# Masked attention: another key block for GpSimd, its product later, and five places instead of four

## The chip, the cores and the metric

The kernel runs on one core of a Trainium2 chip. The metric is the device time of one execution in microseconds (us). Of the kernel before there are three timed runs, with a median of 1539.09 us (1537.86 to 1539.81), and one more execution that was profiled.

The engines by the names of the profile: PE is the matrix engine (PEld its weight loads), DVE the vector engine, ACT the scalar engine, POOL the GpSimd engine, SP the engine that issues most transfers. Each works through its instructions in the order in which they were written out for it.

## The reference

One layer of a diffusion transformer over 1024 latent tokens of width 1024, with 256 context tokens beside them. Two attention branches run on the same tokens: A is windowed (each query sees keys at most 128 tokens away) and B is global; both see all context keys, both have 8 query heads in 2 groups of 4 that share a key head. The change is in A:

```
scores = where(mask, q @ k.T / 8, -inf)      # a block of 128 queries, 3 x 128 keys around it, 256 context keys
m = max(max(scores), sink)
e = exp(scores - m);  p = e / (sum(e) + exp(sink - m))
out = p @ v
```

After the branches come a gated merge, an output projection, a layer norm, a convolutional SwiGLU feed-forward part and a second layer norm. Everything is computed to single precision.

## The kernel before

**Numbers in two parts.** A matrix product takes its operands in a rounded 32-bit form. To keep single precision, a number x is split into a high part (x rounded) and a low part (x minus the high part), and products are summed over the parts.

**Units.** The attention is cut into 32 units: branch (0 is A, 1 is B), block i of 128 queries, key head g. A unit of A in the middle of the sequence has five key blocks of 128: three of the window, and two of the context (numbers 0 to 4); the units of the first and last query block have four. In names, `0_3_1` is branch 0, query block 3, key head 1; `ptl0_3_1_2` is the low part of its block 2.

**A unit's stages.** First scores (`lat`, L507): for each of four heads PE writes scores and mask to PSUM (tile `s`, two places), DVE negates them, bounds them by the sink and finds the maximum (L545), and ACT takes the exponential (L547). One unit later come the values (`value_steps`, L595): one step for each key block. A step (`tr_step`) transposes the block of probabilities for four heads on PE (L604, tile `ptr`, one of three PSUM places of kind `pt` that it shares with two other transposes) and splits it into a high part `pth` and a low part `ptl`. Three steps later (`LAG`), PE multiplies the values with the high part (L627) and with the low part (L628, `av_step`); all blocks of a unit add up in one PSUM place `av`. When the last is in, `out_step` follows: ACT copies `av` out (L639), POOL moves one half (L640), DVE adds the halves (L643), POOL scales the sum (L646) and splits it into the output's two parts (`O`, L84 and L87).

**Who splits a block.** Normally ACT writes the high part from PSUM (L615) and DVE the low part (L616). For the blocks named in `POOL_LO`, ACT copies the block from PSUM to one of two side buffers (L612) and POOL does both parts from there (L84, L87 by way of `split`). In A this holds for one block of each of the eleven units 1_0 to 6_0, block 3 before. Such a block's product is due `PLAG` steps later than the usual three. POOL also splits the queries of a coming unit (`qs`, L84 and L87; it waits there for PE's transpose of an earlier `qs`, L486) and writes a small column (L542).

**What sets the order.** The program lists steps by a table; a scheduler in the language's layer then sets each engine's order from it, and gives tiles their places. `pth` and `ptl` have four places each; a fifth block can only be written when the product of the one that held the place is done. `av_issue` puts the products that are due behind each step.

Of the kernel before, what the change touches and what calls it, by code (L numbers as in the profile page):

```python
# [8 lines left out]
R32 = mybir.dt.float32r  # L9
# [4 lines left out]
P = 128  # L14
# [12 lines left out]
ALPHA = 2.0 ** 0.25  # L27
HALF = 512
FBIG = 3.0e38
POOL_LO = (3,), (2, 6)  # L30
PLAG = 1, 2
VL = 1
NXT = 17
LAG = 3, 3
# [35 lines left out]
def layer_kernel(  # L70
# [9 lines left out]
    def split(src, hi, lo, hi_eng, lo_eng):  # L80
        if hi_eng is nc.scalar:
            nc.scalar.copy(hi, src)  # L82
        elif hi_eng is nc.gpsimd:
            nc.gpsimd.tensor_scalar(out=hi, in0=src, scalar1=1.0, scalar2=0.0, op0=ALU.mult, op1=ALU.add)  # L84
        else:
            hi_eng.tensor_copy(hi, src)
        lo_eng.tensor_tensor(out=lo, in0=src, in1=hi.bitcast(F32), op=ALU.subtract)  # L87
# [378 lines left out]
    class Unit:  # L466
# [128 lines left out]
        def value_steps(self):  # L595
            nm, kt = self.id, self.kt
            vh = self.br * 2 + self.g
            last = self.id == f"1_{NT - 1}_1"
            parts = {}

            def tr_step(n):
                tr = pt_tile(f"ptr{nm}_{n}", R32)
                for h in range(4):
                    i = nc.tensor.transpose(tr[:, h * P:(h + 1) * P], self.bits[:, h, n * P:(n + 1) * P], identr)  # L604
                    tc.add_manual_dep(i.ins, self.owner, data, reason="the row's words are read under another type")
                tr = tr.bitcast(F32)
                hi = att.tile([P, 512], R32, tag="pth", name=f"pth{nm}_{n}", bufs=4)
                lo = att.tile([P, 512], R32, tag="ptl", name=f"ptl{nm}_{n}", bufs=4)
                pooled = n in POOL_LO[self.br] and not last and (self.br or 2 <= 2 * self.i + self.g < 2 * NT - 3)
                if pooled:  # L610
                    rw = side_tile()
                    nc.scalar.copy(rw, tr)  # L612
                    split(rw, hi, lo, nc.gpsimd, nc.gpsimd)
                else:
                    nc.scalar.copy(hi, tr)  # L615
                    nc.vector.tensor_tensor(out=lo, in0=tr, in1=hi.bitcast(F32), op=ALU.subtract)  # L616
                parts[n] = hi, lo
                return pooled

            def av_step(n):  # L620
                first = self.left == len(kt)
                self.left -= 1
                if first:
                    self.av = ps2.tile([P, 512], F32, tag="av", name=f"av{nm}")
                hi, lo = parts.pop(n)
                v = VT[kt[n] // 2][:, kt[n] % 2, vh]
                nc.tensor.matmul(self.av, v, hi, start=first, stop=False)  # L627
                nc.tensor.matmul(self.av, v, lo, start=False, stop=self.left == 0)  # L628

            def out_step():  # L630
                av = self.av
                up = att.tile([HD, 512], F32, tag="up", name=f"up{nm}", bufs=1)
                ot = att.tile([P, 2, P], F32, tag="ot", name=f"ot{nm}", bufs=1)
                if last:
                    low = av
                    nc.scalar.copy(up, av[HD:P])
                else:
                    low = side_tile()
                    nc.scalar.copy(low, av)  # L639
                    nc.gpsimd.tensor_scalar(out=up, in0=low[HD:P], scalar1=1.0, scalar2=0.0, op0=ALU.mult, op1=ALU.add)  # L640
                oe = nc.gpsimd if (self.br or self.i >= NT - 2) and not last else nc.vector
                for h in range(2):
                    oe.tensor_tensor(out=ot[h * HD:(h + 1) * HD],  # L643
                                     in0=low[0:HD].rearrange("p (a b q) -> p a b q", b=2, q=P)[:, :, h],
                                     in1=up.rearrange("p (a b q) -> p a b q", b=2, q=P)[:, :, h], op=ALU.add)
                (nc.vector if last else nc.gpsimd).tensor_tensor(out=ot, in0=ot, in1=self.rb, op=ALU.mult)  # L646
                hf = self.i // 4
                qs = slice((self.i % 4) * P, (self.i % 4 + 1) * P)
                split(ot, otile(self.br, hf, 0, self.g)[:, :, qs], otile(self.br, hf, 1, self.g)[:, :, qs],
                      *((nc.scalar, nc.vector) if last else (nc.gpsimd, nc.gpsimd)))  # L650

            def step(ns):
                pooled = [tr_step(n) for n in ns]
                for n, pl in zip(ns, pooled):
                    clk[0] += 1
                    avq.append((self, n, clk[0] + LAG[self.br] + (PLAG[self.br] if pl else 0)))
                    av_issue()

            self.left = len(kt)
            self.av_step, self.out_step = av_step, out_step  # L660
            g = 1 + self.br
            steps = [lambda n=n: step(range(n, n + g)) for n in range(0, len(kt), g)]
            steps.insert(3 if self.br else 2 if self.i else len(steps), self.rows)
            return steps
# [155 lines left out]
    for n, (gi, k) in enumerate(order):  # L820
# [19 lines left out]
        nm, src, tiles = groups[gi]  # L840
# [40 lines left out]
    def otile(br, hf, hl, g):  # L881
        key = br, hf, hl, g
        if key not in O:
            O[key] = opool.tile([P, 2, HALF], R32, tag="O", name="O%d%d%d%d" % key, bufs=12)
        return O[key]

    att = tc.alloc_tile_pool(name="att", bufs=1, side="right", reuse_waits="tile")
    ps2 = tc.alloc_tile_pool(name="ps2", bufs=1, space=PSUM, reuse_waits="tile")

    def pt_tile(name, dt=F32):  # L890
        return ps2.tile([P, 512], dt, tag="pt", name=name, bufs=3)
# [13 lines left out]
    def side_tile():  # L905
        turn[0] ^= 1
        return side[:, turn[0]]
# [8 lines left out]
    def av_issue(flush=False):  # L916
        while avq:
            u = avq[0][0]
            c = [e for e in avq if e[0] is u and (flush or e[2] <= clk[0])]
            if not c:  # L920
                return
            e = min(c, key=lambda e: e[2])
            avq.remove(e)
            u.av_step(e[1])
            if u.left == 0:
                u.out_step()
# [170 lines left out]
    for f in range(2, KT):  # L1097
# [4 lines left out]
        for hs in halves:  # L1102
            n = HALF * len(hs)
# [246 lines left out]
    for f in (4, 6):  # L1350
        for si in (1, 2):
# [3 lines left out]
            elif f == 6:  # L1355
                (_, st), (_, dg), (_, ca), *ap = ln1(si)
                n = len(pend) - 4
# [587 lines left out]
```

## Time and profile before

| what | us |
|---|---|
| timed runs, median (lowest to highest) | 1539.09 (1537.86 to 1539.81) |
| the profiled execution, its own time | 1537.76 |
| its span, from the first to the last instruction | 1536.0 |
| PE busy in the span | 1507.2 |
| DVE, ACT, POOL busy | 1176.7, 788.3, 749.5 |
| PE idle from 362 to 451 us, where the units with a POOL block are | 9.69 |

The span is 1.76 us shorter than the execution's own time. Branch A's units run from about 333 to 466 us, branch B's to about 733 us; before are projections and gates, after are merge, projection and feed-forward. The matrix clock is granted fully throughout (0.998 in the mean).

A row of the profile's timeline has start, duration, engine, line, operation, out and in, shape, count, and in brackets the idle time ahead of it with what ended that. A row of a group has `| busy, mean ns | idle ahead <- what ended it`. A row of waits has `engine line waited for: us in total, times, longest`. In a row of windows, each engine's busy time stands in the order PE, PEld, DVE, ACT, POOL, then the clock, the transfers' share and GB/s.

### The profile page before, as it was taken

What the parts mean: (1) busy time and instruction counts of PE and PEld (TensorE: products, weight loads), DVE (VectorE), ACT (ScalarE), POOL (GpSimd) and SP (SyncE); (2) the same over time, 40 slices, a digit from 0 to 9 for tenths busy, and PEclk for the clock granted to TensorE, in tenths of its full rate; (3) what the DMA queues carried; (4) which work ended last, traced back from release to release, by engine and by line L of the source; (5) the groups of instructions that cost most, each with busy time, mean ns of one, the idle gap of its engine ahead of it and who ended that gap; (6) DMA issues with size and microseconds to landing.
All of it is one profiled execution on the core that took longest, in us unless ns stands there. A gap on an engine that the chain in (4) does not pass through costs nothing.

```text
span 1536.0 us, 22204 instructions
## 1 busy us (share of the span) xinstructions
PE 1507.2 (98%) x7804; PEld 1263.5 (82%) x7804; DVE 1176.7 (77%) x1761; ACT 788.3 (51%) x1303; POOL 749.5 (49%) x727
## 2 busy tenths in 40 slices
PE   9999999999899999999999999999999999999997
PEld 7888888887777888887888998888888888888887
DVE  6677986638788778878765888888888888657884
ACT  5322222448888777777333554444444444435552
POOL 0356522415667677766123436666667774121121
PEclk9999999999999999999999999999999999999999
DMA  9777672312223677663550322333344447996731
GB/s 371 267 242 247 205 254 87 119 61 70 63 81 82 159 166 154 153 145 87 209 165 24 111 87 96 111 110 110 110 110 110 111 110 229 339 273 210 249 105 55
DMA packets 114399, 232.09 MB, mean 151 GB/s; under 512 B 13200, under 2 KB 28048, under 8 KB 114192
## 3 DMA queue, kind: packets, MB, share of 16 engines
q1 hardware_dynamic: 99056, 201.82, 39.5%
q0 software_dynamic: 10400, 20.19, 8.7%
q10 hardware_dynamic: 4832, 8.68, 1.5%
q8 instruction: 61, 1.00, 0.3%
q14 instruction: 50, 0.41, 0.1%
HBM read 179.45 MB, written 65.86 MB: 160 GB/s over the span
## 4 chain that ended last, share of the span: by engine, by line
PE 88%; POOL 5%; DVE 2%; issue 2%; ACT 2%; DMA 0%; SPq 0%; DVEq 0%; POOLq 0%; ACTq 0%
PE p L90 4%; PE p L91 4%; PE p L92 4%; PE g L90 4%; PE g L91 4%; PE g L92 4%; PE ptr L604 4%; PE av L628 3%; PE av L627 3%; PE b L90 3%; PE b L92 3%; PE b L91 3%; PE c L90 2%; PE c L92 2%; PE d L92 2%; PE c L91 2%
## 5 line engine op out<-in xcount | busy, mean ns | idle before, releaser
L616 DVE TENSOR_TENSOR ptl<-ptr,pth 128x512 fp32r<-128x512 f32 x195 | 128.5, 684 | 28.3 <-ACT pth L615 26.9
L547 ACT ACTIVATE p<-p,nm 128x1280 f32<-128x1280 f32 (+2 forms) x128 | 139.5, 1091 | 12.9 <-DVE p L545 11.9
L615 ACT CAST pth<-ptr 128x512 fp32r<-128x512 f32 x195 | 110.9, 589 | 46.6 <-PE ptr L604 40.3
L87 DVE TENSOR_TENSOR ld<-rd,hd 128x1024 fp32r<-128x1024 f32 x77 | 94.9, 1249 | 51.7 <-ACT hd L82 49.5
L82 ACT CAST hd<-rd 128x1024 fp32r<-128x1024 f32 x77 | 79.4, 1050 | 83.0 <-PE p L92 57.7
L604 PEld LDWEIGHTS ptr<-identr,pb 128*128 128x128 f32 x944 | 97.3, 141 | 21.2 <-ACT pb L550 3.1
L628 PE MATMUL av<-ptl,VT 128*128 128x512 f32 x236 | 98.5, 417 | 10.6 <-POOL ptl L87 10.4
L87 POOL TENSOR_TENSOR wlg<-wg,whg 128x512 fp32r<-128x512 f32 x32 | 48.0, 1510 | 122.2 <-ACT whg L82 83.0
L604 PE MATMUL ptr<-identr,pb 128*128 128x128 f32 x944 | 105.2, 243 | 1.8 <-ACT pb L550 1.2
L90 PE MATMUL p<-hd 128*128 128x512 f32 x264 | 103.5, 392 | 0.0
L627 PE MATMUL av<-pth,VT 128*128 128x512 f32 x236 | 102.2, 433 | 1.2 <-ACT side L639 0.8
L91 PE MATMUL p<-ld,hd 128*128 128x512 f32 x264 | 102.9, 390 | 0.0
L92 PE MATMUL p<-hd,ld 128*128 128x512 f32 x264 | 102.8, 389 | 0.0
L90 PE MATMUL g<-hh,whg 128*128 128x512 f32 x256 | 99.9, 390 | 0.0
L92 PE MATMUL g<-hh,wlg 128*128 128x512 f32 x256 | 99.7, 389 | 0.0
L91 PE MATMUL g<-hl,whg 128*128 128x512 f32 x256 | 99.7, 389 | 0.0
L545 DVE TENSOR_SCALAR_CACHE_REDUCE p<-s,cvt,nmc 128x1024 f32<-128x1024 f32 x64 | 84.0, 1315 | 8.1 <-PE s L497 8.1
L496 PE MATMUL s<-KL,q 128*128 128x512 f32 (+2 forms) x192 | 74.7, 389 | 1.2 <-DVE p L545 1.2
L497 PE MATMUL s<-KL,q 128*128 128x512 f32 (+2 forms) x192 | 72.0, 375 | 0.0
L783 ACT ACTIVATE sg<-g,bgc 128x512 f32<-128x512 f32 x32 | 22.0, 686 | 96.2 <-PE g L92 96.2
L82 ACT CAST wS<-s 128x512 fp32r<-128x512 f32 x76 | 45.3, 620 | 47.5 <-POOL s L1244 46.7
L82 ACT CAST wA<-ru 128x512 fp32r<-128x512 f32 x57 | 35.5, 623 | 63.8 <-PE d L92 34.9
(438 smaller groups left out, 4877.8 us busy)
## 6 DMA issues: line engine op xcount, KB each, us to landing
wml<-in_wmodT_dram SPq DMA_DIRECT2D x48, 512.0 KB
ru<-in_w_up_dram SPq DMA_DIRECT2D x38, 512.0 KB
rd<-td SPq DMA_DIRECT2D x55, 256.0 KB
rd<-sd SPq DMA_DIRECT2D x44, 256.0 KB
rd<-in_w_dn_dram SPq DMA_DIRECT2D x33, 256.0 KB
wm<-in_wmodT_dram SPq DMA_DIRECT2D x16, 512.0 KB
wg<-in_w_g_dram SPq DMA_DIRECT2D x32, 256.0 KB
sgd<-sg ACTq DMA_DIRECT2D x32, 256.0 KB
```

The source lines that it names most:

```text
L82: nc.scalar.copy(hi, src)
L87: lo_eng.tensor_tensor(out=lo, in0=src, in1=hi.bitcast(F32), op=ALU.subtract)
L90: nc.tensor.matmul(ps, a[0], b[0], start=start, stop=False, skip_group_check=resumed)
L91: nc.tensor.matmul(ps, a[0], b[1], start=False, stop=False, skip_group_check=resumed)
L92: nc.tensor.matmul(ps, a[1], b[0], start=False, stop=stop, skip_group_check=resumed)
L545: nc.vector.tensor_scalar(out=out, in0=o, scalar1=self.qscale(nqs)[:, hs] if self.br else -1.0, scalar2=self.other[:, hs], op0=ALU.mult, o ...
L547: nc.scalar.activation(row, row, AF.Exp, bias=self.nm[:, hs], scale=-1.0, accum_out=self.sm[:, hs])
L604: i = nc.tensor.transpose(tr[:, h * P:(h + 1) * P], self.bits[:, h, n * P:(n + 1) * P], identr)
L615: nc.scalar.copy(hi, tr)
L616: nc.vector.tensor_tensor(out=lo, in0=tr, in1=hi.bitcast(F32), op=ALU.subtract)
L627: nc.tensor.matmul(self.av, v, hi, start=first, stop=False)
L628: nc.tensor.matmul(self.av, v, lo, start=False, stop=self.left == 0)
```

## The change

Three numbers change. In A, POOL's block is number 1 of a unit and no longer number 3. Its product is due 3 + 3 = 6 steps after its own step, and no longer 3 + 1 = 4; as block 1 has its step two steps ahead of block 3, both rules come to the same step: the third of the next unit, where block 4 is due too. `pth` and `ptl` have five places each, in both branches. Block 3 is now split by ACT and DVE, block 1 no longer. Which units have a POOL block does not change, nor any instruction's size or the number of instructions in a unit.

```
-POOL_LO = (3,), (2, 6)
-PLAG = 1, 2
+POOL_LO = (1,), (2, 6)
+PLAG = 3, 2
...
-                hi = att.tile([P, 512], R32, tag="pth", name=f"pth{nm}_{n}", bufs=4)
-                lo = att.tile([P, 512], R32, tag="ptl", name=f"ptl{nm}_{n}", bufs=4)
+                hi = att.tile([P, 512], R32, tag="pth", name=f"pth{nm}_{n}", bufs=5)
+                lo = att.tile([P, 512], R32, tag="ptl", name=f"ptl{nm}_{n}", bufs=5)
```

The instructions' order changes with it. PE, around the product of unit 3_1's POOL block (`pth` and `ptl` of 0_3_1_3), before:

```order
L567 MATMUL str0_4_0_4122<-ident_58,sm_0_4_0_3949 4x128
L627 MATMUL av0_3_1_4060<-pth0_3_1_3_4055,VT4_2139 128x512
L628 MATMUL av0_3_1_4060<-ptl0_3_1_3_4056,VT4_2139 128x512
L627 MATMUL av0_3_1_4060<-pth0_3_1_4_4068,VT4_2139 128x512
L604 MATMUL ptr0_4_0_2_4140<-identr_59,pb0_4_0_4012 128x128 x4
L628 MATMUL av0_3_1_4060<-ptl0_3_1_4_4069,VT4_2139 128x512
L486 MATMUL qtr0_5_1_4166<-identr_59,qs0_5_1_4163 128x128 x4
```

The same place now, where the POOL block is 0_3_1_1:

```order
L604 MATMUL ptr0_4_0_1_4095<-identr_59,pb0_4_0_4013 128x128 x4
L628 MATMUL av0_3_1_4060<-ptl0_3_1_3_4057,VT4_2139 128x512
L496 MATMUL s0_4_1_2_4115<-KC_2134,q10_4_1_3920 128x256
L497 MATMUL s0_4_1_2_4115<-KC_2134,q20_4_1_3921 128x256
L567 MATMUL str0_4_0_4123<-ident_58,sm_0_4_0_3947 4x128
L627 MATMUL av0_3_1_4060<-pth0_3_1_1_3974,VT1_2136 128x512
L604 MATMUL ptr0_4_0_2_4141<-identr_59,pb0_4_0_4013 128x128 x4
L628 MATMUL av0_3_1_4060<-ptl0_3_1_1_3975,VT1_2136 128x512
L627 MATMUL av0_3_1_4060<-pth0_3_1_4_4068,VT4_2139 128x512
```

The product of the POOL block stands where it stood, between `str0_4_0` and block 4, but it is another block: 0_3_1_1, which was transposed two steps ahead of 0_3_1_3. The next unit's block 1 (`ptr0_4_0_1`) is transposed in a run of its own, ahead of this product.

POOL between the query parts `qs0_5_1` and the next ones, before:

```order
L84 TENSOR_SCALAR qs0_5_1_4163<-Q0_4_1588 128x4x64
L640 TENSOR_SCALAR up0_2_1_3901<-side_3048 64x512
L87 TENSOR_TENSOR qs0_5_1_4163<-Q0_4_1588,qs0_5_1_4163 128x4x64
L542 TENSOR_SCALAR p0_4_0_3950<-sinkb_64 128x4
L646 TENSOR_TENSOR ot0_2_1_3902<-ot0_2_1_3902,rb0_2_1_3746 128x256
L84 TENSOR_SCALAR O0001_3402<-ot0_2_1_3902 128x2x128
L84 TENSOR_SCALAR pth0_3_0_3_3929<-side_3048 128x512
L87 TENSOR_TENSOR O0011_3403<-ot0_2_1_3902,O0001_3402 128x2x128
L87 TENSOR_TENSOR ptl0_3_0_3_3930<-side_3048,pth0_3_0_3_3929 128x512
```

And now:

```order
L84 TENSOR_SCALAR qs0_5_1_4164<-Q0_4_1588 128x4x64
L640 TENSOR_SCALAR up0_2_1_3902<-side_3048 64x512
L87 TENSOR_TENSOR qs0_5_1_4164<-Q0_4_1588,qs0_5_1_4164 128x4x64
L542 TENSOR_SCALAR p0_4_0_3948<-sinkb_64 128x4
L646 TENSOR_TENSOR ot0_2_1_3903<-ot0_2_1_3903,rb0_2_1_3747 128x256
L84 TENSOR_SCALAR O0001_3403<-ot0_2_1_3903 128x2x128
L87 TENSOR_TENSOR O0011_3404<-ot0_2_1_3903,O0001_3403 128x2x128
L84 TENSOR_SCALAR pth0_3_1_1_3974<-side_3048 128x512
L87 TENSOR_TENSOR ptl0_3_1_1_3975<-side_3048,pth0_3_1_1_3974 128x512
```

Behind the same `qs0_5_1`, POOL now splits a block of unit 3_1, not of 3_0. In the built order, PE has 54 separate runs of transposes (L604, L486) from unit 1_0's first to unit 7_0's first before, and 59 now. Small changes of place also follow in the last units of A and in B; behind the attention PE's order is the same.

## The prediction

> **What bounds the kernel now.** I read the page's busy times first, then the groups, then PE's waits stage by stage, then the timeline around one wait on PE and on POOL. Two lines of the page:
>
> ```profile
> PE 1507.2 (98%) x7804; PEld 1263.5 (82%) x7804; DVE 1176.7 (77%) x1761; ACT 788.3 (51%) x1303; POOL 749.5 (49%) x727
> L628 PE MATMUL av<-ptl,VT 128*128 128x512 f32 x236 | 98.5, 417 | 10.6 <-POOL ptl L87 10.4
> ```
>
> PE is the bound, and of its 29 us of idle time over a third stands ahead of one instruction: the product with a low part that POOL wrote. PE's waits in branch A's stretch (330 to 466 us), then the first row for branch B (466 to 740) and the first for all that comes later:
>
> ```profile
> PE av L628 <- POOL ptl L87: 9.7, 11, 1.3
> PE s L496 <- DVE p L545: 1.2, 4, 0.4
> PE ptr L604 <- ACT pb L550: 0.6, 1, 0.6
> PE av L627 <- ACT side L639: 0.2, 1, 0.2
> ...
> PE av L628 <- POOL ptl L87: 0.7, 1, 0.7
> ...
> PE c L90 <- DVE c L1407: 0.6, 1, 0.6
> ```
>
> Eleven waits, one for each unit of A with a POOL block, 9.7 us together. Nothing behind 466 us makes PE wait for long, so an earlier end of A should move all that follows to an earlier time. By windows (PE, PEld, DVE, ACT, POOL busy):
>
> ```profile
> 345.00:362.00 17.00, 16.54 (x119) 14.13 (x117) 15.09 (x33) 15.22 (x37) 9.33 (x17) 1.00 0.32 84
> 362.00:451.00 89.00, 79.31 (x555) 69.59 (x555) 71.33 (x153) 72.63 (x172) 59.35 (x91) 1.00 0.24 61
> 466.00:480.00 14.00, 12.89 (x79) 10.02 (x78) 13.09 (x27) 12.98 (x24) 10.46 (x18) 1.00 0.23 56
> 500.00:740.00 240.00, 238.47 (x1449) 195.62 (x1448) 188.17 (x363) 168.37 (x291) 162.13 (x203) 1.00 0.60 143
> ```
>
> The second row is the stretch that the change touches: 9.69 us idle in 89, against 0.46 in 17 just ahead of it (the units without a POOL block), and 1.5 in 240 in most of branch B. The third row is where A hands over to B: DVE is busy for 13.09 of 14 us there, and PE is idle for 1.11.
>
> One wait in detail, first PE and then POOL:
>
> ```profile
> 407.00 0.50 PE L628 MATMUL av<-ptl,VT 128*128 128x512 f32 x1 [0.86 <-POOL ptl L87]
> 407.33 0.40 PE L627 MATMUL av<-pth,VT 128*128 128x512 f32 x1
> 407.57 0.46 PE L604 MATMUL ptr<-identr,pb 128*128 128x128 f32 x4
> 407.87 0.47 PE L628 MATMUL av<-ptl,VT 128*128 128x512 f32 x1
> 408.18 0.47 PE L486 MATMUL qtr<-identr,qs 128*128 128x128 f32 x4
> ...
> 409.83 0.39 PE L628 MATMUL av<-ptl,VT 128*128 128x512 f32 x1
> 410.06 0.39 PE L627 MATMUL av<-pth,VT 128*128 128x512 f32 x1
> ...
> 412.79 0.40 PE L627 MATMUL av<-pth,VT 128*128 128x512 f32 x1
> 414.47 0.50 PE L628 MATMUL av<-ptl,VT 128*128 128x512 f32 x1 [1.28 <-POOL ptl L87]
> 414.81 0.80 PE L604 MATMUL ptr<-identr,pb 128*128 128x128 f32 x8
> 415.44 0.41 PE L496 MATMUL s<-KL,q 128*128 128x384 f32 x1
> ```
>
> ```profile
> 408.73 0.40 POOL L84 TENSOR_SCALAR qs<-Q 128x256 fp32r<-128x256 f32 x1 [1.78 <-PE qtr L486]
> 409.22 0.74 POOL L87 TENSOR_TENSOR qs<-Q,qs 128x256 fp32r<-128x256 f32 x1
> 410.05 0.62 POOL L640 TENSOR_SCALAR up<-side 64x512 f32<-64x512 f32 x1
> 411.14 0.47 POOL L542 TENSOR_SCALAR p<-sinkb 128x4 f32<-128x4 f32 x1 [0.48 <-PE ptr L604]
> 411.87 0.62 POOL L84 TENSOR_SCALAR pth<-side 128x512 fp32r<-128x512 f32 x1 [0.26 <-ACT side L612]
> 412.45 0.74 POOL L646 TENSOR_TENSOR ot<-ot,rb 128x256 f32<-128x256 f32 x1
> 413.15 1.27 POOL L87 TENSOR_TENSOR ptl<-side,pth 128x512 fp32r<-128x512 f32 x1
> ```
>
> POOL starts its round when PE has transposed the queries (`qtr`, 408.18, done by 408.65), and needs until 414.42, so 5.8 us, to bring out the low part. PE's next products come earlier than that: the high part's product starts at 412.79, the low one could follow 0.23 later (409.83 to 410.06 shows that step), and stands until 414.47. All that PE has queued behind it stands too: the transposes of the next unit, and so ACT and DVE, who wait for these.
>
> **The change part by part.**
>
> *The wait itself.* The built order shows that POOL's split of 3_1's block 1 stands behind the same `qs0_5_1` as the split of 3_0's block 3 did, so at the same place of POOL's round, one unit ahead. Its product stands where the product of 3_1's block 3 stood, nearly a whole unit of PE time later than in the order before. The first and the last of the eleven waits:
>
> ```profile
> 362.83 0.50 PE L628 MATMUL av<-ptl,VT 128*128 128x512 f32 x1 [0.86 <-POOL ptl L87]
> ...
> 451.39 0.51 PE L628 MATMUL av<-ptl,VT 128*128 128x512 f32 x1 [0.46 <-POOL ptl L87]
> ```
>
> From the one to the other are ten units, 8.86 us for one. POOL was late by 0.9 us in the mean (9.7 by 11) and gets some 8 us more. For PE to stand there still, POOL would have to lose some 7 us, and it has time to spare:
>
> ```profile
> POOL qs L84 <- PE qtr L486: 22.6, 10, 2.8
> ```
>
> That is 2.3 us per unit (362 to 451 us) in which POOL waits for PE at the head of its round. Term: **-9.7**.
>
> *The restart.* The matmul behind a stop comes 0.33 us after it (407.00 to 407.33), in the flow 0.23: 0.1 by 11, **-1.1**.
>
> *More runs of transposes.* By the rows above, four transposes and the first matmul behind them take 0.30 + 0.31 (407.57 to 408.18), of which the matmul alone would be 0.23; eight take 0.63 at once (414.81 to 415.44), with about 0.07 for the matmul behind. Two runs of four cost 0.76, one of eight 0.70. Five more runs: **+0.3**. Bounds: 0, and 5 by 0.38 = 1.9 if each were an added run.
>
> *DVE and ACT come closer to their limits.* Block 3 for block 1 leaves their work the same: 71.33 and 72.63 us in 89, so 7.1 and 7.2 us per unit. A unit of PE without stops is 79.31 us by ten, 7.9; so they would be busy for 90% and 91% of it. Such a load costs PE something, as there are only two places for scores and three for transposes, which DVE's reads set free. The stretch with the nearest load is 345 to 362 us (DVE 89%, ACT 90%): PE idle for 2.7% of it. For 79 us that is **+2.1**. Bounds: nothing, and the 7.9% of the hand-over (DVE 94% busy there), which would be 6.3 us.
>
> *The five places.* The wait for a place is a row of its own, from ACT's waits between 330 and 466 us:
>
> ```profile
> ACT pth L615 <- POOL ptl L87: 1.8, 3, 0.7
> ```
>
> 1.8 us in three cases, on ACT, which is not the bound; PE's 9.7 us are waits for an operand. The Trainium skill, Perfetto Trace Analysis, Optimization Strategy, says that the same gap coming back on the engine that should be saturated can mean that there is no SBUF or PSUM for the next tile, which is a matter of the number of buffers. This speaks against the reading above: by it the fifth place would be the cure and the choice of the block no matter, and by the row above the cure could be worth at most 1.8 us. I take the gain of the places alone as 0, between 0 and 1.8, since with the product six steps behind they are what lets blocks 2 to 4 and the next 0 be written at all. In branch B they can only take waits from ACT, where PE has 1.5 us of idle in 240.
>
> *The hand-over and branch B.* In the last units of A one matmul of scores (`s0_7_1_2`) now stands ahead of `s0_7_0_0` and waits for a place that DVE must have read; the nearest row is PE's wait for such a read, 1.2 us in four cases, the longest 0.4: **+0.4**. In branch B pieces of PE's order trade places with their neighbours; the idle time of A's hand-over and of B (1.1 + 1.5) bounds that at 2 or so either way, and I take 0.
>
> Sum: -9.7 - 1.1 + 0.3 + 2.1 + 0.4 = **-8.0 us**. The profiled execution took 1537.76 (span 1536.0, 1.76 around it), which gives 1529.8; it lies 1.33 below the median of the runs, and against the median of 1539.09 the forecast is **1531.1**. What follows A is bound by PE from 500 us on, and the transfers there are started by buffers that PE sets free, so I let the gain pass in full.
>
> **The rivals.**
>
> *DVE and ACT become A's bound* (0.15). For it: 90% and 91% of load, and DVE's chain per unit has little slack behind the four score reads and four low parts:
>
> ```profile
> L545 DVE TENSOR_SCALAR_CACHE_REDUCE p<-s,negsink 128x640 f32<-128x640 f32 x39 | 33.8, 879 | 9.5 <-PE s L497 9.5
> L616 DVE TENSOR_TENSOR ptl<-ptr,pth 128x512 fp32r<-128x512 f32 x41 | 26.9, 683 | 5.7 <-ACT pth L615 5.7
> ```
>
> Against it: these rows show DVE itself idle for 15 us in that stretch, waiting for PE and for ACT, which in turn waited for PE. With the upper bound of 6.3 in place of 2.1 the time is 1535.3.
>
> *The gap was one of places* (0.05). Then only the fifth place counts, at most 1.8 us: 1537.3. Against it: the timeline has PE's gap end with the very instruction that writes the operand, and places are waited for three times in eleven. This is what the Trainium skill's rule of consistent bubbles would make of the time.
>
> *Slower: PE's new order locks on DVE* (0.10). Transposes of the next unit now stand between the high and low products, each needing one of the three PSUM places that DVE's low part (0.68 us) sets free, behind score reads of 0.88 us. PE stops where such a read is late, and a late PE makes the next scores late. If PE stopped in each unit for one read and half a micro-second more, 1.35 us, that is 14.9 against the 10.8 won: with the other terms +4.5, so 1543.6. It decides for slower from about 0.95 us per unit on. Against it: waits of this kind now are the 1.2 us in four cases above.
>
> *The change doesn't do what it says* (0.06). POOL, which now meets its block behind the same output work as before, might slip a unit behind and be last again; then 1539. Against it: the 2.3 us per unit in which POOL waits.
>
> **How the numbers follow.** The forecast has 0.64. Its own range goes from 1527.1 (no give-back, and the 1.2 us of waits for score reads gone too: -12.0) to about 1535. A measurement of this kernel tells a change from none at about 0.2%, 3 us here, so faster means below 1536.0. The forecast's 0.64 counts as faster, as does 0.12 of the first rival and 0.01 of the places: 0.77. Same: 0.03 of the first, 0.04 of the places, 0.05 of the last: 0.12. Slower: 0.11. The range from 1527.0 to 1537.0 holds nearly all of the forecast's cases, and the first rival's.
>
> **What would show it.** Right: PE's wait at L628 for POOL is gone between 330 and 466 us, the rounds of ten units take about 81 us where they took 89, PE's idle time there is 2 to 3 us and ends with DVE or ACT, and B starts about 8 us earlier and takes as long as it did. POOL still waits at `qs` for PE. The first rival: PE idle for 6 us there, with L545 or L616 as what ended it, and DVE over 93% busy. The slower one: ten units in over 90 us, PE waiting at L604 or L496. The last one: L628 still waits for POOL. Wrong altogether: A shorter by 8 us and the end not earlier, which would mean that something behind it, not PE, sets the time.

## The result, and the profile after

| | before | after |
|---|---|---|
| timed runs, median (lowest to highest), us | 1539.09 (1537.86 to 1539.81) | 1526.76 (1526.08 to 1527.47) |
| the profiled execution, us | 1537.76 | 1526.08 |
| its span, us | 1536.0 | 1524.3 |

The ratio after to before is 0.9921, with a 95% interval of 0.9904 to 0.9938. The medians differ by 12.3 us, the profiled executions by 11.7; the forecast was 8.0. The direction and the place were right. The time lies 0.24 us below the range.

Busy times and the group of the low part's product, from the page after:

```profile
PE 1507.3 (99%) x7804; PEld 1265.9 (83%) x7804; DVE 1177.9 (77%) x1761; ACT 786.5 (52%) x1303; POOL 750.4 (49%) x727
L628 PE MATMUL av<-ptl,VT 128*128 128x512 f32 x236 | 97.6, 413 | 0.6 <-POOL ptl L87 0.3
```

PE's work is the same, 1507.3 us. Its idle time ahead of L628 was 10.6 us, 10.4 of it because of POOL; now it is 0.6, 0.3 of it because of POOL. PE's waits in A's stretch (330 to 454 us) after:

```profile
PE s L496 <- DVE p L545: 0.8, 3, 0.3
PE ptr L604 <- ACT pb L550: 0.5, 1, 0.5
PE av L627 <- ACT side L639: 0.3, 1, 0.3
PE s L496 <- ACT p L547: 0.3, 1, 0.3
```

The eleven waits are gone, and no other took their place: what is left makes 1.9 us, where the rows beside L628 made 2.0 before. Windows of the kernel after (start to end, length, then PE, PEld, DVE, ACT and POOL busy, the clock, the transfers' share, GB/s): the units ahead of POOL's blocks, the stretch that had the waits, A's hand-over to B, and 79 us of the second one for comparison:

```profile
345.00:362.00 17.00, 16.29 (x117) 14.05 (x117) 15.23 (x32) 14.94 (x36) 10.26 (x17) 1.00 0.29 75
362.00:443.00 81.00, 80.49 (x575) 71.93 (x574) 74.14 (x158) 74.98 (x180) 62.34 (x92) 1.00 0.28 71
458.00:472.00 14.00, 13.85 (x90) 11.06 (x88) 13.30 (x28) 12.76 (x24) 11.33 (x18) 1.00 0.13 30
362.00:441.00 79.00, 78.49 (x559) 70.33 (x559) 72.76 (x154) 73.30 (x175) 61.21 (x90) 1.00 0.28 71
```

The same 79 us in the kernel before:

```profile
362.00:441.00 79.00, 69.50 (x482) 60.97 (x482) 63.20 (x136) 63.94 (x152) 52.73 (x81) 1.00 0.25 63
```

PE is idle for 0.51 us in 81, with DVE busy for 92% and ACT for 93% of the time. In the same 79 us, PE now gets through 559 matmuls where it got through 482.

The pace, by POOL's low parts in A (eleven pieces; the two times are the starts of the first and the last), of the kernel before and then after:

```profile
L87 POOL TENSOR_TENSOR ptl<-side,pth x11: 1263/1272/1289, 361.5 to 450.0; 128x512 fp32r<-128x512 f32 x11
```

```profile
L87 POOL TENSOR_TENSOR ptl<-side,pth x11: 1288/1299/1310, 356.5 to 433.0; 128x512 fp32r<-128x512 f32 x11
```

Ten units took 88.5 us and take 76.5. And B's start, by the first and the last of its score products, before and after:

```profile
L496 PE MATMUL sx<-KC,q x64: 276/282/385, 463.2 to 714.0; 128*128 128x256 f32 x64
```

```profile
L496 PE MATMUL sx<-KC,q x64: 275/281/352, 451.5 to 702.4; 128*128 128x256 f32 x64
```

B starts 11.7 us earlier and takes as long (250.8 and 250.9 us), and the span is 11.7 shorter. So the whole gain is made in A, and nothing behind it gives any back. This start of B is the mark by which the experiments below are compared.

The place that stood for the wait, first on PE and then on POOL, after:

```profile
408.84 0.27 PE L567 MATMUL str<-ident,sm 128*4 128x128 f32 x1
408.87 0.48 PE L627 MATMUL av<-pth,VT 128*128 128x512 f32 x1
409.18 0.52 PE L604 MATMUL ptr<-identr,pb 128*128 128x128 f32 x4
409.54 0.46 PE L628 MATMUL av<-ptl,VT 128*128 128x512 f32 x1
```

```profile
402.19 1.30 POOL L87 TENSOR_TENSOR ptl<-side,pth 128x512 fp32r<-128x512 f32 x1
403.85 0.40 POOL L84 TENSOR_SCALAR qs<-Q 128x256 fp32r<-128x256 f32 x1 [0.36 <-PE qtr L486]
```

POOL's low part is done at 403.5 and its product comes at 409.54: it now has 6 us to spare. POOL still waits at `qs` for PE, for 0.36 us here, where it waited 1.78 in the round that the prediction shows.

### The profile page after: what moved, and what is told of

Same layout as the page of the kernel before. It is cut to its first block, busy times and chain, and to the rows that moved or that the text cites. A ratio compares the mean times of both kernels' runs of the same rounds, so it can differ in the third digit from the quotient of the medians.

```text
span 1524.3 us, 22180 instructions
## 1 busy us (share of the span) xinstructions
PE 1507.3 (99%) x7804; PEld 1265.9 (83%) x7804; DVE 1177.9 (77%) x1761; ACT 786.5 (52%) x1303; POOL 750.4 (49%) x727
## 4 chain that ended last, share of the span: by engine, by line
PE 91%; DVE 3%; ACT 2%; issue 1%; DMA 1%; POOL 1%; SPq 0%; DVEq 0%; ACTq 0%; POOLq 0%
PE ptr L604 4%; PE p L90 4%; PE p L92 4%; PE p L91 4%; PE g L90 4%; PE g L92 4%; PE g L91 4%; PE av L627 4%; PE av L628 3%; PE b L90 3%; PE b L91 3%; PE b L92 3%; PE s L496 3%; PE s L497 3%; PE c L90 2%; PE d L90 2%
## 5 line engine op out<-in xcount | busy, mean ns | idle before, releaser
L604 PEld LDWEIGHTS ptr<-identr,pb 128*128 128x128 f32 x944 | 96.4, 140 | 23.7 <-ACT pb L550 3.1
L604 PE MATMUL ptr<-identr,pb 128*128 128x128 f32 x944 | 107.5, 245 | 1.5 <-ACT pb L550 0.9
L628 PE MATMUL av<-ptl,VT 128*128 128x512 f32 x236 | 97.6, 413 | 0.6 <-POOL ptl L87 0.3
L496 PE MATMUL s<-KL,q 128*128 128x512 f32 (+2 forms) x192 | 73.7, 385 | 1.3 <-DVE p L545 0.8
```

The costliest lines, as they stand in the source:

```text
L496: nc.tensor.matmul(o, self.q[0][:, hs], ks, start=True, stop=False)
```

## The experiments

The theory: PE stood still for POOL's low part, once in each of eleven units, and a stop costs more than the idle time that the profile counts (theory W). The rivals: what was short was places for parts (theory P); the gain comes from PE's new order, with the transposes in more separate runs (theory O); or the change cost something through DVE's and ACT's load, and would have won more without it. Each ratio below is to the kernel before, run again beside the version in question; starts, waits and windows come from the one profiled execution of each.

### The places alone

```
-                hi = att.tile([P, 512], R32, tag="pth", name=f"pth{nm}_{n}", bufs=4)
-                lo = att.tile([P, 512], R32, tag="ptl", name=f"ptl{nm}_{n}", bufs=4)
+                hi = att.tile([P, 512], R32, tag="pth", name=f"pth{nm}_{n}", bufs=5)
+                lo = att.tile([P, 512], R32, tag="ptl", name=f"ptl{nm}_{n}", bufs=5)
```

This is the kernel before with the last part of the change alone.

> The kernel before with the five places alone: GpSimd's block is still a unit's fourth, its product one step later than the others. Theory W (the gain is the eleven stops of PE at the product with GpSimd's low part: each costs its idle time, 0.9 us, and about 0.27 us that the idle time doesn't count, for the draining and refilling of the matmul pipe): the stops stay, so 1539 within 2 us, PE's wait for GpSimd at L628 still 9 to 10 us in eleven cases. Theory P (the stops are a matter of places): 1527, no such waits. Theory O (the gain comes from the new order on PE, with the transposes spread out): 1539, as the order stays.

Measured: 1538.58 us, ratio to before 1.0001 (0.9992 to 1.001). PE's wait in A's stretch is what it was:

```profile
PE av L628 <- POOL ptl L87: 9.7, 11, 1.3
```

Five places without the rest are worth nothing.

### The block and the product without the fifth place

```
 POOL_LO = (1,), (2, 6)
 PLAG = 3, 2
-... bufs=5)
+... bufs=4)
```

This is the kernel after with four places for `pth` and `ptl`.

> The change without the fifth place: GpSimd's block is the second, its product six steps later, four places. Theory W: the stops at L628 are gone, 1527 to 1530, where the upper end holds if blocks now wait for places (ACT or GpSimd waiting for PE's product at L615 or L84, some of it passed on to PE). Theory P: 1539, or slower, since one block more is alive than there are places. Theory O: 1527 to 1529, the order of PE in the steady units is nearly the same as in the change.

Measured: 1526.30 us, ratio 0.9917 (0.9903 to 0.9932), so as fast as the change. B starts at 452.4; the 0.9 us to the change's 451.5 go with a lower clock in this one profile, 0.53 and 0.62 in the windows from 340 to 344 us (see the last section). The rows of PE's waits from 330 to 466 us:

```profile
PE s L496 <- DVE p L545: 1.2, 4, 0.4
PE ptr L604 <- ACT pb L550: 0.6, 1, 0.6
```

The fifth place isn't needed either. The two runs together leave nothing of the rival of the places. The rule that the Trainium skill gives for consistent bubbles (Perfetto Trace Analysis, Optimization Strategy), that they can mean too few buffers, did not hold for this one: one more buffer changed the time by a ratio of 1.0001.

### No block for POOL in A

```
-POOL_LO = (1,), (2, 6)
+POOL_LO = (), (2, 6)
```

This is the kernel after with ACT and DVE splitting all blocks of A. What is computed is the same.

> GpSimd splits no block in the masked branch; ACT and VectorE do all five, five places. GpSimd loses 1.9 us of work per unit, VectorE gets 0.68 us more, ACT writes the high part in place of the copy and has the same. Theory W (the stops are all there was): no stop for GpSimd can occur, and with VectorE at 7.75 us per unit the time is 1527.5 to 1531, faster than before by 8 us or more, though no block is moved nor any product. A theory that the block's place or the six steps are worth something by themselves: 1535 or more.

Measured: 1527.51 us, ratio 0.9928 (0.9911 to 0.9944). B starts at 451.1, as early as with the change. The window from 362 to 441 us:

```profile
362.00:441.00 79.00, 78.05 (x565) 69.60 (x564) 75.19 (x167) 73.17 (x175) 39.27 (x71) 1.00 0.27 69
```

With no key block of A coming from POOL the gain is there as well, within the two intervals. So the change won what POOL's lateness cost, and nothing that belongs to block 1 or to the sixth step as such. POOL's help with A's blocks is worth nothing that can be measured here: DVE does the eleven blocks too, is busy for 95% of this window, and PE loses nothing that shows in the time.

This speaks against theory O too. Counted on PE's timeline from A's first score to B's first, the transposes (L604 and L486) stand in 68 separate runs before and 73 with the change, but in 64 here, and the gain is whole. The two kernels with 77 such runs won about half (the product later) and most of it (the product four steps behind), so the number of runs doesn't decide.

### The product earlier still

```
-PLAG = 1, 2
+PLAG = 0, 2
```

This is the kernel before with the POOL block's product due three steps behind its step instead of four: more lateness, and nothing else.

> The kernel before with the product of GpSimd's block no step later than the others (its fourth block, four places). The product comes one step earlier, about 1.5 us, and GpSimd as late as it was. Theory W: longer stops, 2 to 2.5 us idle at L628 in each of eleven units, and a unit takes PE's 7.70 us plus the idle time plus about 0.25: 9.9 to 10.4 in the mean, 1552 to 1558. If the idle time were all that a stop costs, and PE's own pace in the order of before 7.9 us, a unit would take 7.9 plus the idle time. The two differ by 0.05 in a mean unit here; what tells them apart is the order: in the stretches without a stop the units of this kernel show PE's own pace in it.

Measured: 1555.07 us, ratio 1.0101 (1.0086 to 1.0116). B starts at 477.6, 14.4 later than before. PE's two largest rows of waits from 330 to 466 us, and then windows of 20 us (the clock is the number behind POOL's):

```profile
PE av L628 <- POOL ptl L87: 10.3, 10, 1.4
PE av L627 <- POOL pth L84: 7.4, 8, 1.8
```

```profile
400.00:420.00 20.00, 16.71 (x95) 14.46 (x96) 11.99 (x27) 11.63 (x28) 9.36 (x15) 0.83 0.21 55
420.00:440.00 20.00, 17.08 (x119) 14.70 (x117) 14.33 (x31) 15.71 (x39) 11.93 (x19) 1.00 0.21 50
440.00:460.00 20.00, 16.75 (x109) 14.29 (x107) 14.02 (x30) 13.81 (x33) 11.65 (x17) 0.91 0.21 58
```

18 stops and 17.7 us of counted idle time stand where 11 and 9.7 stood: 8.0 more. Seven more stops at 0.27 us for what isn't counted (worked out in the next section) add 1.9. The last part is the clock: the granted share is a mean over the window's 20 us, so 0.83 and 0.91 of it stand for up to 20 x 0.17 + 20 x 0.09 = 5.2 us in which PE was busy without progress (an estimate). The sum of 15.1 is near the 14.4 that B starts later. It doesn't test the 0.27, as the sum without it, 13.2, is nearly as close. From A's first score to B's first PE's busy time is 6.1 us longer than before (124.69 against 118.60), which leaves about 1 us beside the clock for the seven stops. The dose and the loss go together, and the larger dose brings a cost of its own. The four executions of this kernel show that cost as well: the fastest, 1552.49 us, has a mean clock of 0.994, and the slowest, 1556.13 us, 0.991.

### The product later, the block as before

```
-POOL_LO = (1,), (2, 6)
+POOL_LO = (3,), (2, 6)
```

This is the kernel after with block 3 for POOL again, so its product comes two steps later than with block 1: in the next unit's last step.

> The block of before (the fourth) with the product six steps later, five places. Theory W: GpSimd gets two more steps, about 3 us, where it was late by 0.9, so the stops at L628 go and the time is 1527 to 1530. Theory P: 1527. Theory O: the order differs from the change's (two transposes stand in one run again, a unit's last product goes behind the next unit's first transposes), so the gain is smaller than half: 1533 or more. A risk for all: the unit ends three steps later, so its output comes later and the next unit's first product must wait for the one place of the accumulator; if PE waits at L627 for ACT's copy of it, that is 0.3 to 0.6 us by eleven.

Measured: 1532.27 us, ratio 0.9954 (0.9938 to 0.9971). Theory W had expected 1527 to 1530 and missed; theory O's 1533 or more was missed as well, by less. B starts at 457.0: 6.2 us won, about half. PE's waits from 330 to 466 us, one of them on the timeline, and the window from 362 to 441:

```profile
PE ptr L604 <- DVE ptl L616: 3.1, 4, 0.8
PE s L496 <- DVE p L545: 2.1, 8, 0.3
PE ptr L604 <- ACT pb L550: 0.8, 2, 0.5
PE av L628 <- POOL ptl L87: 0.4, 1, 0.4
```

```profile
402.66 0.54 PE L604 MATMUL ptr<-identr,pb 128*128 128x128 f32 x4 [0.71 <-DVE ptl L616]
```

```profile
362.00:441.00 79.00, 74.30 (x528) 65.15 (x526) 65.29 (x144) 69.66 (x164) 54.34 (x86) 1.00 0.26 66
```

POOL is in time here too, and yet half the gain is missing: PE stops at L604 for DVE's reads of `ptr`, and more often at L496. DVE is busy for only 83% of the window, so it isn't full; it is late where PE's new order needs it. These are the waits that the prediction's slower rival named. They came with this place of the product and not with the one that the change took. To move a product later isn't enough: the order of transposes around it counts as well. Which neighbours make the difference was not taken apart further.

### The block early, the product four steps behind

```
-PLAG = 3, 2
+PLAG = 1, 2
```

This is the kernel after with the product two steps earlier.

> The block of the change (the second), its product only one step later than the others as before, five places. Theory W: in the built order GpSimd splits this block ahead of the output work that made it late before, and its product comes some 2 us after; so most stops go, 1527 to 1531, and what is left stands as waits at L628 for GpSimd. If it were the number of steps alone that counts, the stops would stay at 0.9 us and the time at 1539. Theory P: 1527. Theory O: 1527 to 1529.

Measured: 1528.56 us, ratio 0.9933 (0.9919 to 0.9948). B starts at 453.3, so 9.9 of the 11.7 us are won. Two of PE's rows from 330 to 466 us:

```profile
...
PE av L628 <- POOL ptl L87: 0.8, 1, 0.8
...
PE ptr L604 <- DVE ptl L616: 0.7, 1, 0.7
```

Block 1 alone makes POOL early enough in ten units of eleven. Six steps in place of four keep one stop of 0.8 away, and one at L604. Their own worth is small: the intervals of this run and of the change overlap. Beside the kernel with six steps and four places, which was run along with this one, all four times here are longer (1528.43 to 1529.33 against 1525.82 to 1526.59), by 2.3 us in the medians; that the fifth place makes this difference is unlikely, as it was worth nothing above.

### More work on DVE

The next question was the term for DVE's and ACT's load: +2.1 us had been expected, and next to nothing was seen. Each of these kernels adds to the change passes over a block of keys, one or two for each of the eleven units, with results that nobody uses; nothing is left out.

```
             nc.vector.reciprocal(self.sm, self.sm)
+            if not self.br and 2 <= 2 * self.i + self.g < 2 * NT - 3:
+                ...
+                nc.vector.tensor_scalar(out=x, in0=KC[0][:, 0:1].bitcast(F32), scalar1=1.0, scalar2=FBIG,
+                                        op0=ALU.mult, op1=ALU.min, accum_out=xm[:, 0:1])
```

First 256 numbers a row, as here, then 512:

> The change with one more instruction on VectorE in each of the eleven units with a GpSimd block: a pass over 256 numbers per row, some 0.35 us, whose result nobody reads. It measures how near VectorE is to being the bound of the masked branch. Theory F (free): in the change a unit takes 7.70 us, which is PE's own pace, and VectorE is busy for 7.1 of it, so 7.45 still fits and the time stays within 1 us of the change's (1526 to 1528). Theory G (the prediction's term: a load of 90% costs PE some 0.2 us per unit, and more load more): 0.3 us per unit or more, 1530 or more.

> The same with 512 numbers per row, some 0.65 us. VectorE then has 7.75 us of work per unit, more than PE's 7.70. Theory F: only the excess and some friction: units of 7.75 to 8.0, 1527.5 to 1530. Theory G: 0.5 us or more per unit, 1532 or more. In both, PE's waits for VectorE (L496 for the score reads, L604 for the low parts) should show what ends last.

Measured: 1528.27 us, ratio 0.9931 (0.9916 to 0.9946), and 1527.40 us, ratio 0.9925 (0.991 to 0.994). Both missed what they were for. As the passes needed nothing of their unit, the order built from the program put all of them early; the second kernel's group shows where:

```profile
L567 DVE TENSOR_SCALAR_CACHE_REDUCE load<-KC x11: 654/685/687, 336.3 to 373.4; 128x512 f32<-128x512 f32 x11
```

Most of the units in question ran without them. The next two kernels bind each pass to its unit by taking a factor from that unit's sums:

```
             nc.vector.reciprocal(self.sm, self.sm)
+            if 2 <= 2 * self.i + self.g < 2 * NT - 3:
+                x = att.tile([P, 2, NC], F32, tag="load", name=f"load{self.id}", bufs=1)
+                nc.vector.tensor_scalar(out=x, in0=KC[0][:, 0:2].bitcast(F32), scalar1=self.sm[:, 3:4], scalar2=FBIG,
+                                        op0=ALU.mult, op1=ALU.min, accum_out=self.nm[:, 0:1])
```

One pass of 512 a unit, and two (the same instruction twice); lines behind this place are 4 and 6 higher in the rows.

> As the two runs with an extra pass on VectorE, which told nothing, since their extra passes waited for nothing of their unit and all stood ahead of 374 us: here the pass over 512 numbers (0.6 us) takes a factor from its own unit's sum of exponentials, so one stands in each of the eleven units. VectorE's work per unit goes from 7.1 to 7.7 us, PE's pace is 7.70. Theory F (free up to PE's pace): units of 7.7 to 7.9, 1526.5 to 1529. Theory G (90% of load and more costs PE in proportion): units of 8.1 or more, 1531 or more.

> Two such passes per unit, 1.2 us: 8.3 us of VectorE's work, beyond PE's pace. Both theories have VectorE as the bound now: units of 8.3 to 8.6, so 6 to 10 us more than the change, 1533 to 1537, with PE waiting at L496 or L604 for VectorE, and none for GpSimd. If the time stays below 1530, VectorE's work isn't what its busy time says.

Measured: 1529.30 us, ratio 0.9941 (0.9924 to 0.9957), B from 453.6; and 1532.52 us, ratio 0.9961 (0.9946 to 0.9976), B from 457.3. The first lies just above theory F's range and below theory G's, the second just below the range that both gave. With one pass, POOL's low parts, DVE's passes, and the window from 362 to 441 us:

```profile
L87 POOL TENSOR_TENSOR ptl<-side,pth x11: 1290/1293/1304, 356.7 to 435.6; 128x512 fp32r<-128x512 f32 x11
```

```profile
L566 DVE TENSOR_SCALAR_CACHE_REDUCE load<-KC,sm x11: 735/739/746, 354.1 to 430.5; 128x512 f32<-128x512 f32 x11
```

```profile
362.00:441.00 79.00, 77.84 (x551) 68.10 (x550) 74.43 (x169) 71.75 (x171) 58.12 (x90) 1.00 0.27 71
```

With two, POOL's low parts and the same window:

```profile
L87 POOL TENSOR_TENSOR ptl<-side,pth x11: 1286/1292/1305, 356.7 to 438.4; 128x512 fp32r<-128x512 f32 x11
```

```profile
362.00:441.00 79.00, 76.89 (x531) 65.86 (x532) 78.24 (x183) 69.64 (x162) 57.34 (x86) 1.00 0.25 66
```

A unit takes 7.89 us with one pass and 8.17 with two, where the change takes 7.65. DVE's free time in a unit of the change is (79 - 72.76) / 79 of 7.65, so 0.60. One pass of 0.74 is a little more than that and costs 0.24 a unit; two cost 0.52, and DVE is then busy for 99% of the window: it sets the pace. Below its free time DVE's load cost nothing that the runs show (92% in the change, 95% without POOL's blocks). The sizes don't follow a simple limit, though: by that one pass would cost 0.14 and two 0.88. At 94% with one pass there is a loss that isn't there at 95% without POOL, so where in a unit the work stands may count beside its share. Part of the two passes' small price is in DVE's own additions (L643 of the change), which last 0.56 us there in the mean and 0.67 in the change (345 to 441 us), twice in a unit. The rest stays open.

## Why the prediction was right in place and too small in size

The forecast was 8.0 us, and the profiled executions differ by 11.7. By the rows for the whole of A further down, two sizes were wrong. The prediction gave back 2.5 us of idle time, 2.1 of them for the load of DVE and ACT and 0.4 for the hand-over, and 0.3 was seen in A (9.7 less 9.4). And what the stops cost in time that counts as busy was to be 0.8 us (the restart's 1.1, less 0.3 for the transposes) and was 2.4.

**The bound, and where the gain passes to.** Right in kind. The eleven waits went, B started earlier and took as long as before. The sizes went further than described: the ten units were to go from 89 us to 81 and went from 88.5 to 76.5, and PE's idle time there was to be 2 to 3 us and is 0.51 in 79 us.

**The wait itself, -9.7.** The mechanism was right (the places alone 1.0001, without the fifth place 0.9917, without POOL's blocks 0.9928), but the size was taken from counted idle time, and this term was too small. The rows quoted with the prediction held more: the high part's product starts at 412.79, the low one could follow at 413.02 and starts at 414.47. That is 1.45 us lost, where the row counts 1.28. A matmul's record lasts 0.40, but the next one can start 0.23 behind it; idle time begins only when the record ends, so 0.17 of each stop counts as busy. For eleven stops that is 1.9 more (an estimate from this one stop).

The windows show the same without that reasoning. From 362 to 441 us PE's busy time rose by 8.99 us (69.50 to 78.49), but its matmuls by 77, which at 78.49 / 559 = 0.140 us each are 10.8 us. So some 1.8 us of what the kernel before counted as busy in that window was no progress (an estimate, since some records can be missing and the mixture of matmuls isn't quite the same). The Trainium skill, Trainium Kernel Development and Optimization, Best Practices, says to judge the distance from PE's limit by the use of its peak arithmetic and the busy share of weight loads, and not by the busy share of matmuls. The trace agrees for the weight loads: PEld rose from 60.97 to 70.33 us, by which the window before lacked 13.3% of 79 us, 10.5 us, and not 9.

The whole of A shows it with nearly the same work on both sides. From A's first score product to B's first, before and then after:

```profile
332.54:463.24 130.70, 118.60 (x835) 103.11 (x835) 104.72 (x233) 109.33 (x264) 80.06 (x126) 1.00 0.26 70
332.63:451.50 118.87, 116.21 (x831) 102.75 (x831) 105.79 (x232) 107.94 (x259) 82.10 (x125) 1.00 0.29 77
```

Of the 11.8 us by which A is shorter, 9.4 are idle time (12.10 to 2.66) and 2.4 are busy time in which nothing more was done.

**The restart, -1.1.** It wasn't measured apart. With the 0.17 a stop costs 0.27 us beyond its counted idle time, 3.0 us for eleven. The busy time of A fell by 2.4, which has the added runs of transposes in it (+0.3 in the prediction), so the price is about right for these eleven stops. The run with the earlier product doesn't test it, as its clock fell too.

**DVE and ACT come closer to their limits, +2.1.** This step failed. It took the 2.7% of idle time at 345 to 362 us as the price of a load of 90%. In the profile after, the same 17 us have 0.71 us of idle time with DVE at 90%, and the 81 us behind them have 0.51 with DVE at 92%. So that idle time belonged to the place (the first units) and not to the load, which at 92% took no more than these 0.51 us. The added passes showed a cost once they took more than DVE's free time in a unit.

**Five more runs of transposes, +0.3, and the hand-over, +0.4.** They weren't measured apart. The counted waits, their uncounted part and the restarts make 9.7 + 1.9 + 1.1 = 12.7 us, and the profiled executions differ by 11.7. So 1.0 us is left for these two and the load together, where the prediction had 2.8. The hand-over itself runs at 13.85 of 14 us after, against 12.89 before.

**Five places, 0.** Right.

**The execution and the median.** The profiled execution lay 1.33 us below the median before and lies 0.68 below it after. This accounts for the last 0.65 of the 12.3.

**The rivals.** DVE or ACT as the bound: not with the change; two added passes made DVE that. Places: no. PE's new order locking on DVE: not here, but the product at the later place with block 3 brought such waits and cost half the gain. (The sum of that rival, +4.5, has of the other terms only the 0.4; with the 0.3 for the transposes it is 4.8. Nothing else hangs on it.) That the change doesn't do what it says: no. The range's lower end stood for 12.0 us of gain: no give-back and no more waits for score reads, but also without the part of a stop that isn't counted as idle.

None of the versions beats the change: without the fifth place the time is the same (0.9917 against 0.9921, with intervals that overlap).

## What to carry to other kernels

When the engine that bounds the kernel stands again and again ahead of an operand from a helper, ask first where in the helper's round that operand is made, and price a stop by instructions that don't get through (their count in a window, or the weight loads), since the counted idle time leaves out the end of the last matmul and the restart. That an engine beside the bound is 92% busy was no cost in itself here: work out its free time per unit, and charge first what goes beyond it or stands in the way of a particular instruction. And if you move a product, try the neighbouring places too: two that both cured the wait differed by half the gain.

## What the runs showed of the hardware that was not expected

**The clock can halve behind stops of less than 2 us, and doesn't always.** In the run with the earlier product, windows of 2 us show the granted clock at about a half three times. The second case, with the stop ahead of it, the first product behind it, and two of the windows:

```profile
412.51 0.80 PE L627 MATMUL av<-pth,VT 128*128 128x512 f32 x1 [1.83 <-POOL pth L84]
```

```profile
412.00:414.00 2.00, 1.46 (x4) 0.96 (x4) 0.86 (x2) 0.12 (x2) 1.73 (x2) 0.62 0.00 0
414.00:416.00 2.00, 2.00 (x8) 1.90 (x9) 0.87 (x2) 0.00 (x0) 0.00 (x0) 0.53 0.00 0
```

The record of this product lasts 0.80 us where such a record lasts 0.39 to 0.50 otherwise, and after some 3 us it is over. The other two cases, at 402 and 443 us, come behind stops of 0.38 and 1.42 and of 1.73 us. Yet stops of 0.36 and 1.43 us in the same profile, at 431 and 432 us, left the clock at 1.00, and so did those of up to 1.3 us in the kernel before. The run with four places shows the same fall behind much less, four stops of 0.59 us at most between 335 and 339 us; the kernel before has four stops of nearly the same lengths there and no fall. The run with four places, and then the kernel before:

```profile
340.00:342.00 2.00, 2.00 (x12) 1.82 (x10) 1.42 (x4) 1.00 (x2) 0.00 (x0) 0.53 0.32 120
```

```profile
340.00:342.00 2.00, 1.96 (x17) 1.64 (x16) 1.61 (x4) 1.14 (x4) 0.00 (x0) 1.00 0.38 121
```

So the length of a stop doesn't decide alone, and what does isn't shown. The Trainium skill, TensorE: Matmul & The Clock Gate, HAM oscillation, warns of idle gaps over about 3.4 us; here no stop ahead of a fall was longer than 1.83.

**DVE's addition of two buffers and POOL's subtraction slow each other.** DVE adds the halves twice in a unit (L643). Two pairs of additions in the kernel before, and POOL's subtraction for the queries ahead of the first and beside the second:

```profile
410.70 0.85 DVE L643 TENSOR_TENSOR ot<-side,up 64x256 f32<-64x256 f32 x2
...
419.57 1.30 DVE L643 TENSOR_TENSOR ot<-side,up 64x256 f32<-64x256 f32 x2 [0.15 <-POOL up L640]
```

```profile
409.22 0.74 POOL L87 TENSOR_TENSOR qs<-Q,qs 128x256 fp32r<-128x256 f32 x1
...
419.62 0.97 POOL L87 TENSOR_TENSOR qs<-Q,qs 128x256 fp32r<-128x256 f32 x1
```

Apart they last 0.85 and 0.74 us, side by side 1.30 and 0.97. The group of L643 in A, first with the change and then in the run without POOL's blocks:

```profile
L643 DVE TENSOR_TENSOR ot<-side,up x24: 416/592/1477, 349.8 to 436.2; 64x256 f32<-64x256 f32 x24
```

```profile
L643 DVE TENSOR_TENSOR ot<-side,up x24: 404/418/527, 349.8 to 435.6; 64x256 f32<-64x256 f32 x24
```

With the change nearly every pair meets the queries' subtraction, and one addition, the 1.48, a block's own low part. Without POOL's blocks the two mostly lie apart, and an addition lasts at most 0.53. PE lost nothing by it that can be seen: B starts at 451.5 and at 451.1.
